# Squared-ReLU MLP of a hybrid trunk on one NeuronCore: its tile sums all on VectorE, adaLN dot products at other places

## The chip, the core and the metric

One core of a Trainium2 chip runs the whole kernel as one program. The engines are named as in the profile: PE (matrix), DVE (vector), ACT (scalar), POOL (GpSimd) and SP (its queue issues nearly all DMAs). The metric is the device time of one execution in microseconds (us); lower is better.

## The reference, cut to what matters

Two layers work on 1024 latent and 256 context tokens of width 1024. Layer 0 mixes tokens with latent attention, layer 1 with gated linear attention; each layer ends with the MLP. The second layer computes latent tokens alone behind its mixer.

```python
def sqrelu_mlp(h, w1, w2):                    # w1 1024 x 4096, w2 4096 x 1024
    return jnp.square(jax.nn.relu(h @ w1)) @ w2
m_lat = silu_c @ ada_w[i] + ada_b[i]          # 6 vectors of 1024 per layer: shift, scale, gate, twice
h = modulate(rms_norm(x_lat, norm_g[i, 2]), m_lat[:, 3], m_lat[:, 4])
x_lat = x_lat + m_lat[:, 5] * rms_norm(sqrelu_mlp(h, mlp_w1[i], mlp_w2[i]), norm_g[i, 3])
```

Everything is float32. The kernel writes each operand as a high part (a cast, fp32r) and a low part (operand minus high part), and multiplies with three matmuls: high by high, high by low, low by high (`mm3`, L232).

## The kernel before, in words

Activations lie transposed: 128 channels on the partitions, 512 tokens on the free side for each of the two latent blocks, 256 for the context. A tile of 128x512 floats has 256 KB. Weights, hidden tiles and the tiles of `ada_w` come by SP's DMA queue into 12 slots named `stg` (`load`, L212); ACT casts a high part (L204) and DVE or POOL subtracts it from the operand to get the low part (`sub`, L201). `tt` (L888) is the sum or difference of two tiles on the engine that it is given.

The MLP multiplies 2x2 blocks (two halves of the channels by two token blocks) with seven products instead of eight (Strassen's scheme in Winograd's form), so it needs sums of operands, of weights and of results.

`mlp` (L891) runs for each layer:

- `strassen_y` (L949) makes the sums T1 to T4 of the two latent blocks and splits them, in four steps.
- `up_first` (L978) computes the first two products of a pair of hidden tiles ahead, for the first 8 pairs of layer 0 and 11 of layer 1 (`early`), while the second block is still being made ready; the result waits in device memory.
- `up_pair` (L993) runs for each of 16 pairs. An early pair has five products of 12 matmuls (512 columns each), so 60 matmuls; the others have seven, and in layer 0 also the context's products. It makes the sums of weights s1, s2, a21, s2 again, splits five weight tiles (seven or eight in a pair that is not early), adds the products up out of PSUM (always on DVE), squares on ACT, and forms the low operands of the second matrix, t1, t2, c12 and t4, which go to device memory with the hidden tiles. `PLAN['up']` says for each of 16 such operations whether it runs on DVE (V) or POOL (P).
- After pair p, `ada_halves(PLAN['adah'][l][p])` (L257) does so many adaLN coefficients: two loads of 256 KB into `stg` slots, two products with a sum on DVE (L268), the sum of the two (L270), and bias and gain (L273). Its list holds 56 coefficients.
- `down` (L1068) multiplies with the second matrix in five products of 16 steps. In the first two (`w_first`, `w_s3`) a step also multiplies the context in layer 0 (`hc`): 12 matmuls of 512 and 12 of 256 columns. In the other three a step has 12 of 512. Loads and splits run two steps ahead. `ada_halves(1)` follows each step with `p % 3 == 0`.

As written, layer 0 takes 28 coefficients behind its pairs and the other 28 in the five products, so the list is empty before layer 1's MLP.

The order on every engine and on SP's queue is chosen by a list scheduler that simulates the engines' times when the kernel is built, in place of the order of the code; a changed engine or place may so shift the order of the work behind it.

Of the kernel before, what the change touches and what calls it, by code (L numbers as in the profile page):

```python
# [14 lines left out]
ALU = mybir.AluOpType  # L15
# [4 lines left out]
P = 128  # L20
# [70 lines left out]
 'pre': [1, 1, 0],  # L91
 'tk': [0.005, 0.64, 0.0064, 2.5, 1.024, 2.5],
 'gla': 'v2 s2 h2 h0 g0 v0 g2',
 'adah': [[0, 2, 3, 3, 2, 2, 2, 3, 2, 2, 2, 0, 0, 2, 2, 1], [0, 2, 2, 2, 2, 2, 2, 2, 2, 2, 2, 2, 2, 2, 2, 0]],
 'yield': [[[3.0, 6.0, 1.3, 8.0, 8.4, 1.3], [3.0, 8.4, 1.3, 8.0, 6.0, 1.3], [3.0, 6.0, 1.3, 8.0, 6.0, 1.3],
# [7 lines left out]
 'last': [3.0, 4.0, 1.3],  # L103
 'ladd': [3, 5, 6, 7],
 'up': [['VVPPVVVVVPPVVPPP', 'VVPPVVVPVVPVPPPP'], ['VVPVVVVPVVPPPPPP', 'PPPPVPPVVPVPPPPP']]}


def bits(ap):
# [3 lines left out]
class Trunk:  # L112
# [834 lines left out]
        self.nc.sync.dma_start(self.hidc_scr[f], self.sq_relu(ps, CTX))  # L947

    def strassen_y(self, ops, x, y):  # L949
        V, Pl, S = self.nc.vector, self.nc.gpsimd, ALU.subtract  # L950
        for k in range(4):
            t1, t2, t3, t4 = (self.t() for _ in range(4))
            self.tt(Pl, t1, y[k], x[k], S)
            self.tt(V, t2, y[k + 4], t1, S)
            self.tt(Pl, t3, y[k + 4], y[k], S)
            self.tt(Pl, t4, x[k + 4], t2, S)
            for n, t in (("22", y[k + 4]), ("T2", t2), ("T1", t1), ("T3", t3), ("T4", t4)):
                ops[n].append(self.msplit(t, 512, V))
            yield
# [32 lines left out]

    def up_pair(self, l, p, B, hc, early):  # L993
        nc, I = self.nc, self.I
        V, Pl = nc.vector, nc.gpsimd
        U = [Pl if x == 'P' else V for x in PLAN['up'][l][early]]
        if early:
            hc = None
        a11, a12 = (self.load(I["w1"][l, 2 * p, i]) for i in range(2))
        a21, a22 = (self.load(I["w1"][l, 2 * p + 1, i]) for i in range(2))  # L1000
        s1, s2 = self.slot("s", 512), self.slot("s", 512)
        w = {} if early else {"11": self.wsplit(a11, U[0]), "12": self.wsplit(a12, U[1])}
        self.tt(U[2], s1, a21, a22, ALU.add)
        self.tt(U[3], s2, s1, a11, ALU.subtract)
        w["S2"] = self.wsplit(s2, U[4])
        w["S1"] = self.wsplit(s1, U[5])
        if hc:
            w["21"] = self.wsplit(a21, U[6])
        self.tt(U[7], a21, a11, a21, ALU.subtract)
        w["S3"] = self.wsplit(a21, U[8])  # L1010
        w["22"] = self.wsplit(a22, U[9])
        self.tt(U[10], s2, a12, s2, ALU.subtract)
        w["S4"] = self.wsplit(s2, U[11])

        if early:
            c12, c11 = self.load(self.a_scr[l, p]), self.load(self.hid_scr[l][p, 0])
        else:
            c12, c11 = self.top_left(w, B)
        c22, c21 = self.t(), self.t()
        ps = self.product(w["S2"], B["T2"])  # L1020
        self.tt(V, c12, ps, c12, ALU.add)
        if hc:
            self.up_ctx_part(2 * p, (w["11"], w["12"]), hc)
        ps = self.product(w["S3"], B["T3"])
        self.tt(V, c21, ps, c12, ALU.add)
        ps = self.product(w["S1"], B["T1"])
        self.tt(V, c22, ps, c21, ALU.add)
        self.tt(V, c12, ps, c12, ALU.add)
        ps = self.product(w["S4"], B["22"])
        self.tt(V, c12, ps, c12, ALU.add)  # L1030
        if hc:
            self.up_ctx_part(2 * p + 1, (w["21"], w["22"]), hc)
        ps = self.product(w["22"], B["T4"])
        self.tt(V, c21, ps, c21, ALU.add)
        for c in (c22, c21, c12) if early else (c11, c22, c21, c12):
            self.square_relu(c)
        out = self.hid_scr[l][p]

        def put(i, x):
            nc.sync.dma_start(out[i], x)  # L1040

        t1, t2, t4 = self.t(), self.t(), self.t()
        if not early:
            put(0, c11)
        put(4, c22)
        put(5, c21)
        self.tt(U[12], t1, c12, c11, ALU.subtract)
        put(3, t1)
        self.tt(U[13], t2, c22, t1, ALU.subtract)
        put(1, t2)  # L1050
        self.tt(U[14], c12, c22, c12, ALU.subtract)
        put(2, c12)
        self.tt(U[15], t4, c21, t2, ALU.subtract)
        put(6, t4)

    def w2(self, l, f, i, tag="stg"):
# [11 lines left out]
    def down(self, l, C, yc):  # L1068


        nc = self.nc
        V = nc.vector
        keep, later = {}, []

        def part(p, r, i):
            return self.w2(l, 2 * p + r, i)

        def s3(p, a11):
            keep[p] = self.m()
            self.tt(V, keep[p], a11, part(p, 0, 1), ALU.subtract)  # L1080

        def s1(p, a21):
            self.tt(V, keep[p], a21, part(p, 1, 1), ALU.add)

        def w_first(p):
            a11 = part(p, 0, 0)
            w = self.wsplit(a11, V)
            s3(p, a11)
            return w, w

        def w_s3(p):
            w = self.wsplit(keep[p], V)
            a21 = part(p, 0, 1)
            s1(p, a21)
            return w, self.wsplit(a21, V) if yc is not None else None

        def w_s1(p):
            w = self.wsplit(keep[p], V)
            self.tt(V, keep[p], keep[p], part(p, 0, 0), ALU.subtract)
            return w, None  # L1100

        def w_s2(p):
            w = self.wsplit(keep[p], V)
            self.tt(V, keep[p], part(p, 1, 0), keep[p], ALU.subtract)
            return w, None

        def w_s4(p):
            return self.wsplit(keep.pop(p), V), None

        def copied(name):  # L1110
            def put(n, ps):
                C[name, n] = self.m()
                nc.scalar.copy(C[name, n], ps)
            return put

        def sums(n, ps):
            u = C["12", n] = self.m()
            self.tt(V, u, ps, C["11", n], ALU.add)
            later.extend(((C["u3", n], C["u3", n], u), (u, u, C["22", n]), (C["22", n], C["22", n], C["u3", n])))

        def last(n, ps):
            self.tt(V, C["12", n], ps, C["12", n], ALU.add)

        stages = ((w_first, 0, copied("11"), 0), (w_s3, 2, copied("u3"), 4), (w_s1, 3, copied("22"), None),
                  (w_s2, 1, sums, None), (w_s4, 4, last, None))
        steps = [(s, p) for s in stages for p in range(NP)]

        def prepare(s, p):
            (w, wc), hc = s[0](p), None
            b = self.msplit(self.load(self.hid_scr[l][p, s[1]]), 512, V)  # L1130
            if yc is not None and s[3] is not None:
                hc = self.msplit(self.load(self.hidc_scr[2 * p]), CTX, V)
            return w, b, wc, hc

        ready = [prepare(*x) for x in steps[:2]]
        for i, (s, p) in enumerate(steps):
            w, b, wc, hc = ready.pop(0)
            if i + 2 < len(steps):
                ready.append(prepare(*steps[i + 2]))
            if p == 0:  # L1140
                pss = [self.ps() for _ in range(4)]
                psc = [self.ps() for _ in range(2)] if hc else []
            for n in range(4):
                self.mm3(pss[n], self.cols(w, n * P), b, p == 0, p == NP - 1)
                if p == NP - 1:
                    s[2](n, pss[n])
            for n in range(4 if hc else 0):

                self.mm3(psc[n // 2][:, (n % 2) * CTX:(n % 2) * CTX + CTX], self.cols(wc, n * P), hc,
                         p == 0 and n % 2 == 0, p == NP - 1, True)  # L1150
                if p == NP - 1:
                    self.into_ctx(yc, s[3] + n, psc[n // 2][:, (n % 2) * CTX:(n % 2) * CTX + CTX])
            if p % 3 == 0:
                self.ada_halves(1)
            if later:
                self.tt(V, *later.pop(0), ALU.add)
# [508 lines left out]
```

## Time and profile before

| what | value |
|---|---|
| time, median of 3 runs | 2968.3 us (2967.92 to 2971.18) |
| profiled execution: time, span | 2972.39 us, 2970.6 us |
| mean granted clock of PE in it | 0.969 |
| busy share PE, DVE, ACT, POOL | 93%, 76%, 54%, 37% |
| DMA | 535.48 MB, mean 180 GB/s |

Busy time counts the union of an engine's instructions; neighbours on DVE overlap, so the pitch from start to start can be less than a duration. The granted clock is a share of full speed, 2.4 GHz; the lower level is 1.2 GHz. In time: layer 0's early pairs run from about 940 to 1100 us, its other pairs to 1290, the two products with the context to 1420, the other three to 1550; layer 1's early pairs from about 2390 to 2560, its other pairs to 2650, its five products to 2860.

### The profile page before, as it was taken

The page shows a single profiled execution, that of the slowest core. Times are in us where ns is not written, and L with a number is a line of the kernel's source. Part 1 is how long each engine was busy: PE and PEld are TensorE (multiplying, and loading weights), DVE is VectorE, ACT ScalarE, POOL GpSimd, SP SyncE. Part 2 cuts the span into 40 slices and gives each one's busy share as a digit, 9 for nine tenths or more (in the row PEclk, how much of TensorE's full clock was granted, in tenths as well). Part 3 has the DMA queues.
Part 4 walks back from the last instruction along what each step waited for, and adds up shares of the span by engine and source line. Part 5 has one row for each costly group of instructions (what it writes and reads, how often), then busy time and mean ns, then how long its engine had stood idle before and what let it go on. Part 6 is the DMA issues. An engine that isn't in the chain of part 4 may idle for free. (4 is left out here: it accounts for less than half of the span.)

```text
span 2970.6 us, 44564 instructions
## 1 busy us (share of the span) xinstructions
PE 2761.4 (93%) x14646; PEld 2358.3 (79%) x14646; DVE 2265.1 (76%) x4048; ACT 1603.6 (54%) x3360; POOL 1092.3 (37%) x757
## 2 busy tenths in 40 slices
PE   6799898999989889999999999799889999999997
PEld 4678887898778768888787888688887778788877
DVE  8898989887788985576878673466897876577666
ACT  4577665756555344444445464656655644555443
POOL 5554444522004763310002232356561289620012
PEclk8999999999999999999999999899999999999999
DMA  6221433324545774486765565667585647577454
GB/s 206 67 78 63 128 105 129 105 73 167 194 157 171 251 251 141 148 303 202 256 200 177 166 203 171 212 207 229 186 275 206 209 149 242 174 274 263 140 177 157
DMA packets 319384, 535.48 MB, mean 180 GB/s; under 512 B 33072, under 2 KB 96432, under 8 KB 319152
## 3 DMA queue, kind: packets, MB, share of 16 engines
q1 hardware_dynamic: 313328, 527.39, 54.0%
q10 hardware_dynamic: 5760, 5.25, 0.5%
q8 instruction: 115, 1.88, 0.3%
q14 instruction: 117, 0.96, 0.1%
q0 software_dynamic: 64, 0.00, 0.0%
HBM read 412.18 MB, written 120.32 MB: 179 GB/s over the span
## 5 line engine op out<-in xcount | busy, mean ns | idle before, releaser
L235 PE MATMUL ps<-m,w 128*128 128x512 f32 (+1 forms) x2320 | 906.7, 392 | 20.7 <-DVE m L201 20.2
L236 PE MATMUL ps<-m,w 128*128 128x512 f32 (+1 forms) x2320 | 899.2, 391 | 28.3 <-DVE w L201 22.5
L234 PE MATMUL ps<-m,w 128*128 128x512 f32 (+1 forms) x2320 | 891.4, 394 | 30.1 <-ACT m L204 13.2
L234 PEld LDWEIGHTS ps<-m,w 128*128 128x128 f32 x2320 | 445.1, 193 | 124.6 <-ACT m L204 18.9
L236 PEld LDWEIGHTS ps<-m,w 128*128 128x128 f32 x2320 | 445.5, 193 | 123.6 <-DVE w L201 28.3
L235 PEld LDWEIGHTS ps<-m,w 128*128 128x128 f32 x2320 | 447.1, 193 | 115.9 <-DVE m L201 28.1
L201 POOL TENSOR_TENSOR w<-stg,w 128x512 fp32r<-128x512 f32 (+2 forms) x157 | 220.4, 1406 | 818.5 <-ACT w L204 747.2
L204 ACT CAST w<-stg 128x512 fp32r<-128x512 f32 (+2 forms) x510 | 310.0, 615 | 310.0 <-PE ps L235 233.6
L201 DVE TENSOR_TENSOR w<-stg,w 128x512 fp32r<-128x512 f32 x353 | 280.5, 798 | 154.0 <-ACT w L204 136.5
L204 ACT CAST m<-stg 128x512 fp32r<-128x512 f32 x296 | 177.8, 625 | 153.6 <-DMA stg<-hid 139.7
L201 DVE TENSOR_TENSOR m<-stg,m 128x512 fp32r<-128x512 f32 x244 | 173.7, 724 | 55.1 <-ACT m L204 53.9
L234 PE MATMUL ps<-m,m 128*128 128x256 f32 (+1 forms) x632 | 187.3, 316 | 29.5 <-ACT m L204 18.6
L235 PE MATMUL ps<-m,m 128*128 128x256 f32 (+1 forms) x632 | 195.6, 311 | 10.4 <-POOL m L201 5.9
L234 PE MATMUL ps<-c,w 128*128 128x256 f32 (+1 forms) x664 | 186.4, 288 | 16.6 <-ACT c L436 7.1
L236 PE MATMUL ps<-m,m 128*128 128x256 f32 (+1 forms) x632 | 192.0, 305 | 1.8 <-DVE m L427 1.8
L235 PE MATMUL ps<-c,w 128*128 128x256 f32 (+1 forms) x664 | 185.4, 283 | 5.9 <-DVE c L437 3.5
L236 PE MATMUL ps<-c,w 128*128 128x256 f32 (+1 forms) x664 | 184.7, 283 | 0.0
L968 ACT ACTIVATE t<-t 128x512 f32<-128x512 f32 x109 | 68.8, 631 | 205.2 <-DVE t L889 197.6
L889 DVE TENSOR_TENSOR t<-ps,t 128x512 f32<-128x512 f32 x164 | 111.2, 684 | 86.2 <-PE ps L236 51.4
L234 PEld LDWEIGHTS ps<-m,m 128*128 128x128 f32 x632 | 123.7, 197 | 40.3 <-ACT m L204 20.2
L889 POOL TENSOR_TENSOR t<-t,t 128x512 f32<-128x512 f32 x82 | 124.3, 1525 | 73.0 <-DVE t L889 29.3
L234 PEld LDWEIGHTS ps<-c,w 128*128 128x128 f32 x664 | 125.4, 192 | 22.0 <-ACT c L436 7.5
(309 smaller groups left out, 6132.2 us busy)
## 6 DMA issues: line engine op xcount, KB each, us to landing
stg<-in_mlp_w SPq DMA_DIRECT2D x256, 256.0 KB, 4.0
stg<-hid SPq DMA_DIRECT2D x227, 256.0 KB, 3.7
hid<-t SPq DMA_DIRECT2D x205, 256.0 KB, 3.3
stg<-in_w SPq DMA_DIRECT2D x182, 256.0 KB, 3.2
ada<-in_adaT SPq DMA_DIRECT2D x88, 512.0 KB, 3.7
stg<-in_adaT SPq DMA_DIRECT2D x112, 256.0 KB, 3.7
stg<-in_gla_wv SPq DMA_DIRECT2D x64, 256.0 KB, 3.8
stg<-in_mla_wo SPq DMA_DIRECT2D x48, 256.0 KB, 4.4
```

Of the source, the lines that this page charges most:

```text
L201: eng.tensor_tensor(out=out, in0=a, in1=bits(hi), op=ALU.subtract)
L204: self.nc.scalar.copy(hi, src)
L234: mm(ps, lhs[0], rhs[0], start=first, stop=False, skip_group_check=shared)
L235: mm(ps, lhs[0], rhs[1], start=False, stop=False, skip_group_check=shared)
L236: mm(ps, lhs[1], rhs[0], start=False, stop=last, skip_group_check=shared)
L889: eng.tensor_tensor(out=out, in0=a, in1=b, op=op)
L968: self.nc.scalar.activation(c, c, AF.Relu)
```

## The change

Every sum of weights, every low half and every low operand of the first matrix runs on DVE, in `strassen_y` and in `up_pair` (the subtractions of L201 follow the engine given). `PLAN['up']` is gone. The dot products of layer 0's first eight pairs are gone, the last eight have two each, and in `down` one follows every step of a product with the context (32 in layer 0), none in the other three. Eight coefficients are left for layer 1, where pairs 1 to 4 take two each. In `down` of layer 1 the list is empty.

```diff
- 'adah': [[0, 2, 3, 3, 2, 2, 2, 3, 2, 2, 2, 0, 0, 2, 2, 1], [0, 2, 2, 2, 2, 2, 2, 2, 2, 2, 2, 2, 2, 2, 2, 0]],
+ 'adah': [[0, 0, 0, 0, 0, 0, 0, 0, 2, 2, 2, 2, 2, 2, 2, 2], [0, 2, 2, 2, 2, 2, 2, 2, 2, 2, 2, 2, 2, 2, 2, 0]],
- 'up': [['VVPPVVVVVPPVVPPP', 'VVPPVVVPVVPVPPPP'], ['VVPVVVVPVVPPPPPP', 'PPPPVPPVVPVPPPPP']]}
...
-            self.tt(Pl, t1, y[k], x[k], S)
+            self.tt(V, t1, y[k], x[k], S)
-            self.tt(Pl, t3, y[k + 4], y[k], S)
-            self.tt(Pl, t4, x[k + 4], t2, S)
+            self.tt(V, t3, y[k + 4], y[k], S)
+            self.tt(V, t4, x[k + 4], t2, S)
...
-        U = [Pl if x == 'P' else V for x in PLAN['up'][l][early]]
-        w = {} if early else {"11": self.wsplit(a11, U[0]), "12": self.wsplit(a12, U[1])}
-        self.tt(U[2], s1, a21, a22, ALU.add)
+        w = {} if early else {"11": self.wsplit(a11, V), "12": self.wsplit(a12, V)}
+        self.tt(V, s1, a21, a22, ALU.add)
... (U[3] to U[15] become V in the same way)
-            if p % 3 == 0:
+            if hc or yc is None and p % 3 == 0:
                 self.ada_halves(1)
```

## Rows read from the trace of the kernel before

**Rows 1.** The page, busy time and share of each engine, instructions.

```profile
PE 2761.4 (93%) x14646; PEld 2358.3 (79%) x14646; DVE 2265.1 (76%) x4048; ACT 1603.6 (54%) x3360; POOL 1092.3 (37%) x757
```

**Rows 2.** Stretches by stage; columns as in the first line.

```profile
core 0: us, PE busy (x) PEld busy (x) DVE busy (x) ACT busy (x) POOL busy (x), PEclk, DMA share, GB/s
940.00:1080.00 140.00, 121.39 (x492) 96.36 (x491) 126.57 (x211) 55.25 (x98) 96.73 (x61) 0.94 0.72 236
1100.00:1280.00 180.00, 179.65 (x950) 155.37 (x951) 107.67 (x182) 80.53 (x140) 64.12 (x46) 0.99 0.48 159
1290.00:1420.00 130.00, 126.90 (x720) 110.92 (x719) 88.47 (x191) 55.11 (x110) 3.37 (x1) 0.99 0.77 254
1420.00:1550.00 130.00, 127.18 (x559) 104.66 (x558) 111.07 (x237) 58.68 (x108) 1.28 (x1) 0.99 0.72 234
2380.00:2560.00 180.00, 170.80 (x723) 137.49 (x721) 120.36 (x140) 81.60 (x144) 156.07 (x108) 0.97 0.61 196
2660.00:2840.00 180.00, 180.00 (x796) 149.05 (x795) 126.68 (x198) 83.23 (x144) 0.00 (x0) 1.00 0.63 209
```

**Rows 3.** A stretch of 20 us in the first context product, same columns.

```profile
1340.00:1360.00 20.00, 20.00 (x118) 17.70 (x117) 10.12 (x21) 10.01 (x21) 0.00 (x0) 1.00 0.47 149
```

**Rows 4.** PE's waits, layer 0's early pairs (936 to 1100 us): total, times, longest.

```profile
PE ps L236 <- DVE w L201: 17.6, 8, 4.5
```

**Rows 5.** PE's waits in layer 1's early pairs, 2390 to 2560 us.

```profile
PE ps L236 <- POOL w L201: 5.8, 2, 4.4
```

**Rows 6.** Waits of SP's queue, 940 to 1100 us.

```profile
SPq L214 <- DVE y L268: 46.3, 32, 4.3
```

**Rows 7.** Waits of SP's queue, 1290 to 1420 us.

```profile
SPq L214 <- DVE y L268: 14.0, 15, 2.7
```

**Rows 8.** POOL in order of time: start, us, instruction.

```profile
1018.07 1.29 POOL L889 TENSOR_TENSOR stg<-stg,stg 128x512 f32<-128x512 f32 x1
```

**Rows 9.** DVE in order of time at the same place.

```profile
1018.10 1.81 DVE L268 CUSTOM_DVE_ANT_0 stg<-stg,cl 128x512 f32<-128x512 f32 x1 [2.49 <-DMA stg<-in_adaT]
```

**Rows 10.** DVE in order of time, POOL idle, third product of layer 0.

```profile
1494.69 0.69 DVE L201 TENSOR_TENSOR w<-m,w 128x512 fp32r<-128x512 f32 x1
1495.30 0.15 DVE L270 TENSOR_TENSOR m<-y 128x1 f32<-128x1 f32 x1
1495.37 0.69 DVE L201 TENSOR_TENSOR m<-stg,m 128x512 fp32r<-128x512 f32 x1
...
1497.78 0.69 DVE L268 CUSTOM_DVE_ANT_0 stg<-stg,cl 128x512 f32<-128x512 f32 x1
...
1498.39 0.69 DVE L201 TENSOR_TENSOR w<-m,w 128x512 fp32r<-128x512 f32 x1
...
1499.60 0.22 DVE L283 SCALAR_TENSOR_TENSOR m<-m,vec 128x1 f32<-128x1 f32 x1
1499.73 0.69 DVE L268 CUSTOM_DVE_ANT_0 stg<-stg,cl 128x512 f32<-128x512 f32 x1
```

**Rows 11.** DVE in order of time, first context product: a 256-column split.

```profile
1308.26 0.42 DVE L201 TENSOR_TENSOR c<-stg,c 128x256 fp32r<-128x256 f32 x1
1308.60 0.68 DVE L268 CUSTOM_DVE_ANT_0 stg<-stg,cl 128x512 f32<-128x512 f32 x1
```

**Rows 12.** Groups of DVE, 920 to 1100 us: busy, mean ns, idle before.

```profile
L268 DVE CUSTOM_DVE_ANT_0 stg<-stg,cl 128x512 f32<-128x512 f32 x46 | 47.5, 1042 | 16.7 <-DMA stg<-in_adaT 14.7 <-DMA hid<-t 1.8
L201 DVE TENSOR_TENSOR w<-s,w 128x512 fp32r<-128x512 f32 x27 | 26.3, 979 | 0.6 <-ACT w L204 0.4
```

**Rows 13.** DMA over 1290 to 1330 us.

```profile
DMA packets 8498, 13.90 MB, mean 348 GB/s; under 512 B 947, under 2 KB 2518, under 8 KB 8494
```

**Rows 14.** A group of POOL, 1100 to 1280 us (eight pairs of layer 0).

```profile
L889 POOL TENSOR_TENSOR t<-t,t 128x512 f32<-128x512 f32 x21 | 29.9, 1439 | 27.3 <-DVE t L889 14.0 <-issue 11.8 <-POOL t L889 1.5
```

More of the change, by code (lines that the diff above doesn't have):

```diff
@@ L103 @@
  'last': [3.0, 4.0, 1.3],
- 'ladd': [3, 5, 6, 7],
- 'up': [['VVPPVVVVVPPVVPPP', 'VVPPVVVPVVPVPPPP'], ['VVPVVVVPVVPPPPPP', 'PPPPVPPVVPVPPPPP']]}
+ 'ladd': [3, 5, 6, 7]}
 def bits(ap):
@@ L949, in strassen_y @@
     def strassen_y(self, ops, x, y):
-        V, Pl, S = self.nc.vector, self.nc.gpsimd, ALU.subtract
+        V, S = self.nc.vector, ALU.subtract
         for k in range(4):
             t1, t2, t3, t4 = (self.t() for _ in range(4))
-            self.tt(Pl, t1, y[k], x[k], S)
+            self.tt(V, t1, y[k], x[k], S)
             self.tt(V, t2, y[k + 4], t1, S)
-            self.tt(Pl, t3, y[k + 4], y[k], S)
-            self.tt(Pl, t4, x[k + 4], t2, S)
+            self.tt(V, t3, y[k + 4], y[k], S)
+            self.tt(V, t4, x[k + 4], t2, S)
             for n, t in (("22", y[k + 4]), ("T2", t2), ("T1", t1), ("T3", t3), ("T4", t4)):
@@ L994, in up_pair @@
         nc, I = self.nc, self.I
-        V, Pl = nc.vector, nc.gpsimd
-        U = [Pl if x == 'P' else V for x in PLAN['up'][l][early]]
+        V = nc.vector
         if early:
@@ L1001, in up_pair @@
         s1, s2 = self.slot("s", 512), self.slot("s", 512)
-        w = {} if early else {"11": self.wsplit(a11, U[0]), "12": self.wsplit(a12, U[1])}
-        self.tt(U[2], s1, a21, a22, ALU.add)
-        self.tt(U[3], s2, s1, a11, ALU.subtract)
-        w["S2"] = self.wsplit(s2, U[4])
-        w["S1"] = self.wsplit(s1, U[5])
-        if hc:
[L1008 to L1013, printed above, removed]
+        w = {} if early else {"11": self.wsplit(a11, V), "12": self.wsplit(a12, V)}
+        self.tt(V, s1, a21, a22, ALU.add)
+        self.tt(V, s2, s1, a11, ALU.subtract)
+        w["S2"] = self.wsplit(s2, V)
+        w["S1"] = self.wsplit(s1, V)
+        if hc:
+            w["21"] = self.wsplit(a21, V)
+        self.tt(V, a21, a11, a21, ALU.subtract)
+        w["S3"] = self.wsplit(a21, V)
+        w["22"] = self.wsplit(a22, V)
+        self.tt(V, s2, a12, s2, ALU.subtract)
+        w["S4"] = self.wsplit(s2, V)
         if early:
@@ L1046, in up_pair @@
         put(5, c21)
-        self.tt(U[12], t1, c12, c11, ALU.subtract)
+        self.tt(V, t1, c12, c11, ALU.subtract)
         put(3, t1)
-        self.tt(U[13], t2, c22, t1, ALU.subtract)
+        self.tt(V, t2, c22, t1, ALU.subtract)
         put(1, t2)
-        self.tt(U[14], c12, c22, c12, ALU.subtract)
+        self.tt(V, c12, c22, c12, ALU.subtract)
         put(2, c12)
-        self.tt(U[15], t4, c21, t2, ALU.subtract)
+        self.tt(V, t4, c21, t2, ALU.subtract)
         put(6, t4)
```

## The prediction

> **What bounds the kernel now.** The page first: PE is busy for 93% of the span, DVE for 76%, POOL for 37% [rows 1]. A change that takes no matmul away can move the time only where PE stands still or runs at the low clock. So the stretches by stage come next, and in them the count of matmuls, since PE's busy time is no rate. In layer 1's products, at full clock and with nothing idle, 796 matmuls of 512 columns take 180 us, 0.226 us each [rows 2]. By that pitch each stage has a loss, idle time and low clock together:
>
> - layer 0's early pairs, 940 to 1080 us: 140 - 492 x 0.226 = 28.8 us, clock 0.94 [rows 2];
> - layer 1's early pairs with their start, 2380 to 2560: 180 - 723 x 0.226 = 16.6 us [rows 2];
> - the products with the context, 1290 to 1420: 118 matmuls, half of each width, fill 20 us [rows 3], so a step of 24 takes 4.07 us; 720 are 30 steps, 122.1 us, and 7.9 us are lost [rows 2];
> - the other three products of layer 0: 130 - 559 x 0.226 = 3.7 us [rows 2] (the few narrower matmuls make it a little more);
> - the other pairs of layer 0, 1100 to 1280: PE busy for 179.65 of 180 us [rows 2], nothing to win.
>
> Then the waits: in layer 0's early pairs PE waited 17.6 us for low parts of weights from DVE [rows 4], in layer 1's 5.8 us for those of POOL [rows 5].
>
> **What a DVE operation costs.** With POOL idle a split is followed 0.61 us later by the next instruction, and 0.60 to 0.61 us separates neighbours although each lasts 0.69 [rows 10]: I count 0.605 us for a 128x512 operation, 0.34 for a 256-column one [rows 11], and for one adaLN coefficient two products of 0.61, a sum of 0.07 and a correction of 0.13 [rows 10], 1.42 us. Beside POOL it is otherwise: at 1018.07 POOL starts 1.29 us of work, DVE's product starts 0.03 us later and lasts 1.81 [rows 8, 9], that is until 0.55 us after POOL's end. In the early pairs the splits of sums average 0.979 us and the products 1.042 [rows 12]. POOL's work thus lengthens DVE's.
>
> **The change, part by part.**
>
> *Early pairs of layer 0.* An early pair has 5 splits, 4 sums of weights, 4 low operands and 6 sums out of PSUM on DVE: 19 x 0.605 = 11.5 us, against PE's 60 x 0.226 = 13.56. Now it holds 11 of these, stretched, and 17 coefficients over eight pairs; measured, 126.57 us for 492 matmuls are 15.4 us per pair [rows 2], more than PE's. The coefficients go from here, and with them 14.7 us in which DVE stood with a product at its head whose load was late [rows 12], and 46.3 us in which SP's queue waited for DVE to give back such a slot [rows 6], with the next weights behind it. What is late next is the chain sum, cast, split of a pair's first weights, and the start, where 12 operand sums (7.3 us) come to DVE. Bounds: the whole 28.8 us goes; or, if each pair gets the 3.4 us of waits on DVE that POOL had per pair in rows 14, DVE is at 14.9 instead of 15.4 us and 8 x 0.5 = 4 us go. I take 20, nearer the upper end, since the longest waits on DVE here were for the loads that go: -20 us.
>
> *Other pairs of layer 0.* 23 operations of 512 columns, two of 256 and two coefficients: 13.9 + 0.7 + 2.8 = 17.4 us of DVE per pair; eight pairs have 180 us of PE [rows 2], about 22.5 each. Hidden beside PE's matmuls: 0. Without that cover the seven operations from POOL would cost 4.2 us a pair.
>
> *Early pairs of layer 1.* POOL is at 156.07 of 180 us [rows 2] and PE's wait for it, 5.8 us [rows 5], goes. DVE has again 11.5 us per pair, 14.3 in the four pairs that get two coefficients: 0.8 us too much in each, and their loads take slots. Bounds: 16.6 us gained if all loss goes; or 4 us more lost than now (four pairs at 0.8, no gain). I take -2, near the second end, because the load on DVE there rises from 120.36/723 x 60 = 10.0 us per pair.
>
> *Products with the context.* 32 coefficients instead of 12. A step of the first product has three 512-wide operations and one narrow: 2.15 + 1.42 = 3.57 us of DVE against 4.07; of the second, four and one: 2.76 + 1.42 = 4.18, so 102%. A step loads 896 KB, and 512 KB with a coefficient: 1.44 MB, 46.1 MB in 32 steps; at 348 GB/s, reached over 40 us here [rows 13], 132.5 us, against PE's 130.2. But a step then takes six of twelve slots, and SP's queue already waits 14.0 us for products to return slots [rows 7]. Bounds: from below, all loss gone, -7.9; from above, the queue's mean rate of this stage, 254 GB/s [rows 2], 46.1 / 0.254 = 181.5 us, 51.3 over PE, +43 against now. I take 16 to 17 lost instead of 7.9, nearer the rate of rows 13, where the queue was kept full: +9 us.
>
> *Other three products of layer 0.* A step has three operations, 1.8 us, of PE's 2.7, with no coefficient left: 3.7 lost becomes about 1: -3 us.
>
> *Sum.* -20 - 2 + 9 - 3 = -16 us. The profiled execution took 2972.4 us (its span of 2970.6 and 1.8 around it), 4.1 over the median of the runs (2968.3); it becomes 2956.4, and a median about 2952.
>
> **A rule against it.** The Trainium skill (Perfetto Trace Analysis, Optimizing Scalar/DVE Operations) says that of a saturated DVE some work may well be given to another engine, even GPSIMD; this change does the reverse where DVE is busiest. The same place warns that the two share a read port, so that moving work between them may not help. This trace bears out the warning [rows 8, 9]; what the first half would make of the time is rival C.
>
> **The rivals.**
>
> *B, slower: the slots of the context products decide.* Queue and DVE wait on each other: a load needs a slot, a slot needs DVE's product, DVE waits in order for loads. If the queue gives no more than its present 254 GB/s [rows 2], the stage costs +43, and the sum is -25 + 43 = +18: 2986. It decides from where the stage loses 25 us more than now, a step of 5.1 us, 282 GB/s. For it: [rows 7]; against: [rows 13].
>
> *C, slower: DVE stays as slow per operation as now, and gets more.* Layer 0's early pairs: 15.4 + 8 x 0.605 - 2.1 x 1.42 = 17.3 us against 13.56, 30 us over eight pairs, nothing gained. Layer 1's: 10.0 + 9 x 0.605 + 1.0 = 16.4 us, 2.9 x 11 = 32 instead of 16.6 lost. +1 + 15 + 9 - 3 = +22: about 2990. Against it: durations fall to 0.69 as soon as POOL is idle [rows 10].
>
> *D, no change: waits move into DVE's line.* POOL's low operands waited 27.3 us in eight pairs [rows 14], 3.4 us a pair; there nobody stood behind them, on DVE the next pair's splits do. 11.5 us leave room for 2.1; at 2.7 us each of 19 early pairs loses 0.6, 12 us: 2964. For it: DVE runs in order; against: layer 0's early pairs lose such waits with their coefficients.
>
> *E, more:* all loss of rows 2's early pairs and three products goes, and the context stage stays as it is: -49, 2919.
>
> **How the numbers follow.** Chances: forecast 0.49 (own range 2938 to 2961), B 0.18, C 0.07, D 0.13, E 0.13. About 0.2%, 6 us, is what a measurement can tell from no change. Faster: forecast and E, 0.62 in all. Same: 0.13, most of D and the weak end of B. Slower: 0.25, the rest of B, C and D. The range 2925 to 2985 leaves out the far ends of E, B and C.
>
> **What would show it.** Right: POOL near 0 in the MLP's pairs; L201's w<-s near 0.69 us; over 85% as many matmuls per us in layer 0's early pairs as in rows 2's last stretch, now 79%; a context stage of 140 to 150 us with SP's waits for L268 doubled. Wrong: an early pair above 14.5 us (C or D), or a context step above 5.1 us (B).

## The result and the profile after

The changed kernel takes 2920.8 us (median of four runs, 2915.4 to 2923.2), the kernel before 2969.7 in the same series: a ratio of 0.983, 95% interval 0.981 to 0.985, and 0.983 again (0.982 to 0.985) in a second series of experiment 11. That is 49 us less where 16 were forecast, outside the range; it is the total that rival E priced at 2919. Medians are of fast runs; one execution of experiment 1, of 6949 us, is left out. The profiled executions are 57 us apart (2972.4 and 2915.4), since that of the changed kernel was the fastest of its runs; sums by stage go with these 57.

The busy time of the page, as in [rows 1]:

```profile
PE 2746.1 (94%) x14646; PEld 2354.7 (81%) x14646; DVE 2313.1 (79%) x4331; ACT 1603.9 (55%) x3360; POOL 664.0 (23%) x474
```

DVE has 283 instructions more and POOL 283 fewer, but DVE's busy time grew by only 48 us, 0.17 us for each.

The stretches that answer to [rows 2] (layer 0's early pairs; the products with the context, from the last hidden tile of the context to the last copy of the second product; the three others; layer 1's early pairs; behind the first, part of layer 0's other pairs):

```profile
core 0: us, PE busy (x) PEld busy (x) DVE busy (x) ACT busy (x) POOL busy (x), PEclk, DMA share, GB/s
940.00:1080.00 140.00, 140.00 (x653) 117.24 (x652) 123.77 (x228) 66.56 (x119) 0.00 (x0) 1.00 0.67 219
1100.00:1250.00 150.00, 150.00 (x799) 129.70 (x798) 112.18 (x221) 67.22 (x120) 0.00 (x0) 1.00 0.55 180
...
1253.00:1396.00 143.00, 140.94 (x794) 121.91 (x793) 125.51 (x322) 64.38 (x130) 0.00 (x0) 1.00 0.93 316
...
1386.00:1516.00 130.00, 129.76 (x574) 107.26 (x575) 91.73 (x151) 59.90 (x108) 3.20 (x3) 1.00 0.56 185
2340.00:2520.00 180.00, 178.68 (x777) 146.21 (x776) 164.64 (x293) 90.92 (x156) 0.00 (x0) 0.99 0.69 227
```

In layer 0's early pairs PE is never idle and at full clock; before it lost a fifth of the time. (The early pairs now end sooner, so the 653 matmuls hold narrower ones of the pairs behind them.) POOL is at 0. DVE's groups there, 940 to 1080 us, answer to [rows 12] (line numbers are one or two lower in the changed kernel):

```profile
L200 DVE TENSOR_TENSOR w<-s,w 128x512 fp32r<-128x512 f32 x27 | 18.3, 681 | 1.1 <-ACT w L203 1.1
...
L267 DVE CUSTOM_DVE_ANT_0 stg<-stg,cl 128x512 f32<-128x512 f32 x13 | 8.9, 689 | 3.6 <-DMA stg<-in_adaT 3.4
```

0.979 us has become 0.681 and 1.042 has become 0.689. (The 13 products belong to later pairs.) SP's waits for these products to return a slot, in 940 to 1080 us, are 13.0 us, where [rows 6] had 46.3 over a slightly longer stretch; in the products with the context they fell from the 14.0 of [rows 7] to 4.9, though there are more than twice as many of them. First the early pairs', then the context stage's:

```profile
SPq L213 <- DVE y L267: 13.0, 10, 2.8
```

```profile
SPq L213 <- DVE y L267: 4.9, 17, 0.9
```

To see where the 57 us are, some events of the program that both have serve as marks: the first and the last time that a tile is written or read. Each line has them behind its durations ("first to last start"). Kernel before:

```profile
L984 SPq DMA_DIRECT2D hid<-t x19: 319/327/433, 852.6 to 2384.7; - x19
L947 SPq DMA_DIRECT2D hidc<-t x32: 319/379/2222, 872.6 to 1289.3; - x32
L1246 ACT COPY m<-ps x8: 363/377/397, 1349.7 to 1431.3; 128x256 f32<-128x256 f32 x8
L214 SPq DMA_DIRECT2D s<-x_scr x48: 319/424/1112, 1530.7 to 2889.6; - x48
L982 SPq DMA_DIRECT2D a_scr<-t x19: 319/326/461, 847.7 to 2376.8; - x19
L1040 SPq DMA_DIRECT2D hid<-t x186: 319/370/1951, 966.0 to 2648.5; - x186
```

The changed kernel:

```profile
L983 SPq DMA_DIRECT2D hid<-t x19: 319/320/385, 854.5 to 2336.4; - x19
L946 SPq DMA_DIRECT2D hidc<-t x32: 319/382/848, 874.9 to 1253.5; - x32
L1244 ACT COPY m<-ps x8: 360/376/405, 1316.0 to 1395.7; 128x256 f32<-128x256 f32 x8
L213 SPq DMA_DIRECT2D s<-x_scr x48: 319/427/1667, 1489.1 to 2834.0; - x48
L981 SPq DMA_DIRECT2D a_scr<-t x19: 319/320/446, 849.6 to 2332.1; - x19
L1038 SPq DMA_DIRECT2D hid<-t x186: 319/327/2132, 963.9 to 2596.4; - x186
```

Between these marks:

| stretch | from, to | before | after | difference | forecast |
|---|---|---|---|---|---|
| layer 0's first matrix | first hid, last hidc | 436.7 | 399.0 | -37.7 | -20 |
| products with the context | last hidc, last copy L1246 | 142.0 | 142.2 | +0.2 | +9 |
| the other products, end of layer 0 | that, first read of x_scr | 99.4 | 93.4 | -6.0 | -3 |
| layer 1's mixer and start of its MLP | that, last a_scr | 846.1 | 843.0 | -3.1 | 0 |
| layer 1's pairs | that, last hid | 271.7 | 264.3 | -7.4 | -2 |

Up to the first mark the changed kernel is 1.9 us later. The 3.1 us of layer 1's mixer, where nothing was changed, stay open. Behind the last mark it is 4.9 us shorter, but those belong to layer 1's pairs: the mark is a store that comes from DVE's line, and that line now runs further behind PE. Counted by PE's own work, the same matmuls in the same mix of widths, the early pairs are these (columns as above): 750 matmuls of layer 0, before and after; 794 of layer 1, before, after, and in run 8 below, which leaves no coefficient to layer 1:

```profile
925.50:1118.50 193.00, 169.82 (x750) 137.42 (x749) 166.51 (x277) 78.41 (x141) 125.29 (x81) 0.94 0.69 225
```

```profile
928.20:1084.50 156.30, 156.30 (x750) 131.82 (x749) 140.05 (x257) 74.19 (x134) 0.00 (x0) 1.00 0.65 212
```

```profile
2368.50:2568.50 200.00, 187.75 (x794) 150.77 (x793) 136.48 (x154) 95.28 (x170) 174.75 (x120) 0.97 0.60 193
```

```profile
2323.90:2511.70 187.80, 184.14 (x794) 149.02 (x793) 173.75 (x314) 94.69 (x163) 0.00 (x0) 0.99 0.67 222
```

```profile
2324.10:2507.10 183.00, 181.44 (x794) 148.12 (x794) 165.22 (x271) 94.62 (x164) 0.00 (x0) 1.00 0.65 211
```

So layer 0's early pairs gained 36.7 us, nearly all of its stretch's 37.7, and layer 1's 12.2, not 7.4.

### The profile page after: what moved, and what is told of

It reads as the page before. It is cut to its first block, busy times and chain, and to the rows that moved or that the text cites. A ratio compares the mean times of both kernels' runs of the same rounds, so it can differ in the third digit from the quotient of the medians.

```text
span 2913.6 us, 44354 instructions
## 1 busy us (share of the span) xinstructions
PE 2746.1 (94%) x14646; PEld 2354.7 (81%) x14646; DVE 2313.1 (79%) x4331; ACT 1603.9 (55%) x3360; POOL 664.0 (23%) x474
## 5 line engine op out<-in xcount | busy, mean ns | idle before, releaser
L234 PE MATMUL ps<-m,w 128*128 128x512 f32 (+1 forms) x2320 | 897.5, 388 | 13.2 <-DVE m L200 13.2
L233 PE MATMUL ps<-m,w 128*128 128x512 f32 (+1 forms) x2320 | 882.2, 390 | 25.2 <-ACT m L203 14.5
L235 PE MATMUL ps<-m,w 128*128 128x512 f32 (+1 forms) x2320 | 889.7, 387 | 2.1 <-DVE w L200 2.0
L200 POOL TENSOR_TENSOR w<-stg,w 128x512 fp32r<-128x512 f32 (+2 forms) x138 | 194.1, 1409 | 1706.2 <-ACT w L203 1648.3
L233 PEld LDWEIGHTS ps<-m,w 128*128 128x128 f32 x2320 | 439.4, 190 | 118.8 <-ACT m L203 21.8
L234 PEld LDWEIGHTS ps<-m,w 128*128 128x128 f32 x2320 | 442.0, 191 | 103.8 <-DVE m L200 18.3
L235 PEld LDWEIGHTS ps<-m,w 128*128 128x128 f32 x2320 | 440.1, 190 | 91.6 <-DVE w L200 4.4
L200 DVE TENSOR_TENSOR w<-stg,w 128x512 fp32r<-128x512 f32 x372 | 273.1, 738 | 142.6 <-ACT w L203 127.8
L233 PE MATMUL ps<-m,m 128*128 128x256 f32 (+1 forms) x632 | 187.9, 316 | 28.7 <-ACT m L203 17.7
L234 PE MATMUL ps<-m,m 128*128 128x256 f32 (+1 forms) x632 | 198.0, 315 | 7.4 <-DVE m L200 4.1
L235 PE MATMUL ps<-m,m 128*128 128x256 f32 (+1 forms) x632 | 194.9, 310 | 2.4 <-DVE m L426 2.4
L233 PEld LDWEIGHTS ps<-m,m 128*128 128x128 f32 x632 | 124.0, 197 | 39.8 <-ACT m L203 19.7
L203 ACT CAST w<-m 128x512 fp32r<-128x512 f32 x128 | 79.2, 622 | 117.1 <-PE ps L234 116.9
L234 PEld LDWEIGHTS ps<-m,m 128*128 128x128 f32 x632 | 125.2, 198 | 17.6 <-POOL m L200 5.5
```

The source lines that it names most:

```text
L200: eng.tensor_tensor(out=out, in0=a, in1=bits(hi), op=ALU.subtract)
L203: self.nc.scalar.copy(hi, src)
L233: mm(ps, lhs[0], rhs[0], start=first, stop=False, skip_group_check=shared)
L234: mm(ps, lhs[0], rhs[1], start=False, stop=False, skip_group_check=shared)
L235: mm(ps, lhs[1], rhs[0], start=False, stop=last, skip_group_check=shared)
```

## The experiments

Two theories stood against each other. P: POOL's work lengthened DVE's. S: the dot products' late loads and the slots that they held were the loss. Below, "layer 0's stretch" and "layer 1's stretch" are the first and last row of the table, read in each trace from the same marks; for layer 1 the text gives the count by matmuls beside it.

| run | median us | ratio to before, 95% | layer 0's stretch | context products | layer 1's stretch |
|---|---|---|---|---|---|
| 1, sums on DVE alone | 2927.6 | 0.987 (0.985 to 0.990) | 415.9 | 140.9 | 262.6 |
| 2, dot products moved alone | 2947.8 | 0.994 (0.991 to 0.996) | 406.6 | 141.0 | 281.0 |
| 3, POOL reads 512 columns | 2995.7 | 1.009 (1.007 to 1.012) | 446.1 | 142.2 | 299.4 |
| 4, POOL reads 16 columns | 2913.0 | 0.982 (0.979 to 0.984) | 398.8 | 144.0 | 262.8 |
| 5, early loads | 2923.7 | 0.984 (0.982 to 0.986) | 404.2 | 141.6 | 264.0 |
| 6, early DVE work | 2930.2 | 0.987 (0.984 to 0.989) | 412.3 | 141.5 | 263.9 |
| 7, POOL writes only | 2919.3 | 0.983 (0.981 to 0.985) | 398.6 | 137.8 | 263.4 |
| 8, none in layer 1 | 2909.4 | 0.980 (0.977 to 0.982) | 401.0 | 139.5 | 261.8 |
| 9, context: more DVE work | 2939.7 | 0.990 (0.988 to 0.993) | 397.6 | 155.9 | 263.8 |
| 10, context: more loads | 2938.4 | 0.989 (0.985 to 0.993) | 401.0 | 154.8 | 263.9 |

**1 and 2: each half alone.** The first is the changed kernel with the list and the condition of before:

```diff
- 'adah': [[0, 0, 0, 0, 0, 0, 0, 0, 2, 2, 2, 2, 2, 2, 2, 2], ...
+ 'adah': [[0, 2, 3, 3, 2, 2, 2, 3, 2, 2, 2, 0, 0, 2, 2, 1], ...
-            if hc or yc is None and p % 3 == 0:
+            if p % 3 == 0:
```

> All sums and low halves on DVE as in the changed kernel; the adaLN dot products at their old places (17 behind layer 0's early pairs, one behind every third step of the five products). Theory P (POOL's work lengthened DVE's operations in the early pairs, and that was the loss): most of the 49 us between the two kernels is here, 2920 to 2932 us. DVE then has 11.5 us plus 2.1 x 1.42 = 14.5 us per early pair of layer 0 against PE's 13.56, some 8 us lost there, nothing else. Theory S (the dot products' late loads and their slots were the loss): at most the 6 us of PE's waits for POOL in layer 1 come back, 2955 to 2968 us, and SP's queue still waits some 46 us for L268 between 940 and 1100 us.

The second is the kernel before with the opposite two lines.

> The other half alone: dot products moved as in the changed kernel, the sums divided between DVE and POOL as before. Theory P: an early pair of layer 0 still has DVE operations of about 1 us beside POOL, 11 of them against 13.56 us of PE, so it falls under PE's time and part of the loss goes, 2945 to 2962 us; layer 1's pairs with coefficients get slower. Theory S: the early pairs of layer 0 run at PE's rate, 38 us earlier at their end as in the changed kernel, 2925 to 2938 us.

Their stretches of 940 to 1080 us, columns as above, first the one with all sums on DVE, then the one with the dot products moved:

```profile
940.00:1080.00 140.00, 128.58 (x562) 104.35 (x561) 131.98 (x295) 57.90 (x101) 0.00 (x0) 0.98 0.76 251
```

```profile
940.00:1080.00 140.00, 135.17 (x615) 111.88 (x615) 107.98 (x155) 68.99 (x119) 106.32 (x71) 0.99 0.65 216
```

In the same order, PE's wait for DVE in 940 to 1100 us, and for the second run its splits of sums in 940 to 1080:

```profile
PE ps L233 <- DVE t L888: 8.6, 4, 3.9
```

```profile
PE ps L236 <- DVE w L201: 2.4, 1, 2.4
L201 DVE TENSOR_TENSOR w<-s,w 128x512 fp32r<-128x512 f32 x27 | 26.7, 993 | 5.0 <-ACT w L204 5.0
```

By the total time both fall where P had them. By stage neither theory is whole. In layer 0's stretch sums on DVE alone bring 20.8 us and moved dot products alone 30.1, together 37.7: the halves overlap. Run 1 takes away most of DVE's excess but not all of it: 131.98 us for 562 matmuls are 14.1 for the 60 of a pair, against PE's 13.56. In the second run DVE's splits are still lengthened (w<-s at 0.993 us), yet DVE, at 108 of 140 us, has room, and PE waited for DVE's low parts for 2.4 us in one place, against [rows 4]'s 17.6. Some 7 us of loss stay, though (163.5 us for the 750 matmuls counted above, against 156.3). In layer 1 only P's half gains, 9.1 us by the marks and 17.0 by matmuls (183.0 us, as run 8), and coefficients beside divided sums cost 9.3 by the marks, 12.5 by matmuls.

**3, 4 and 7: what of POOL's work holds DVE up.** In every pair POOL does extra work whose results nobody reads, in three forms:

```diff
+        for hi, lo in w.values():      # run 3; run 4 has 16 in place of 512
+            self.tt(nc.gpsimd, s1[:, :512], bits(hi)[:, :512], bits(lo)[:, :512], ALU.add)
+        for _ in w:                    # run 7
+            nc.gpsimd.memset(s1, 0.0)
```

> The changed kernel, and in every pair of the first matrix POOL adds the high and low part of each split weight tile (512 columns, five per early pair), into the tile of s1, which nobody reads any more: extra work, its results unused. Theory P: DVE's operations with two operands in SBUF are stretched again beside these, by about 0.5 us for each of POOL's, 2.5 us on 11.5 per early pair; with the waits the early pairs lose 5 to 25 us: 2926 to 2946 us, and w<-s averages over 0.85 us. If the port does nothing: 2921 us, w<-s at 0.69.

> The control for it: the same additions on POOL with the same waits, but on 16 columns of 512, so that POOL holds nothing for long. Theory P: 2918 to 2925 us, as the changed kernel. If it was the waits and longer-held weight and s tiles that cost time beside wide POOL work, and not the port, this one is as slow as with 512 columns.

> The changed kernel, and POOL sets the tile of s1 to zero once for every split weight tile (five times per early pair, 512 columns), when nobody reads it any more: POOL writes SBUF and reads nothing; extra work, unused. If only POOL's reads hold up DVE's operations with two operands in SBUF: 2913 to 2924 us, w<-s at 0.68 us as in the changed kernel. If any POOL work on SBUF does, as the wide additions did: 2930 us or more, w<-s over 0.75.

DVE in 940 to 1080 us beside wide reads:

```profile
L200 DVE TENSOR_TENSOR w<-s,w 128x512 fp32r<-128x512 f32 x24 | 20.1, 843 | 0.0
L200 DVE TENSOR_TENSOR w<-stg,w 128x512 fp32r<-128x512 f32 x18 | 18.6, 1043 | 0.0
L888 DVE TENSOR_TENSOR stg<-ps,stg 128x512 f32<-128x512 f32 x24 | 16.2, 678 | 0.0
```

POOL there, and then POOL in the run that only writes, with DVE's splits beside it:

```profile
L888 POOL TENSOR_TENSOR s<-w,w 128x512 f32<-128x512 f32 x42 | 66.3, 1579 | 72.6 <-DVE w L200 69.4 <-DVE m L282 2.0
```

```profile
L1014 POOL MEMSET s<- 128x512 f32 x48 | 25.3, 527 | 115.5 <-DVE w L200 113.2
```

```profile
L200 DVE TENSOR_TENSOR w<-s,w 128x512 fp32r<-128x512 f32 x27 | 18.3, 683 | 1.2 <-ACT w L203 1.2
```

Reads of 512 columns lengthen DVE's splits, which have two SBUF operands, to 0.84 and 1.04 us on average, leave its additions with a PSUM operand at 0.678, and cost 75 us, far more than the 5 to 25 expected for the early pairs: my sum had 0.5 us for each of five, but DVE's room beside PE in an early pair is only 2 us (13.56 less 11.5), and both layers lost, 47 us in layer 0's stretch and 35 in layer 1's. The same waits with 16 columns cost nothing, nor does POOL when it writes without reading. So it is the reading, and not POOL's being late with tiles. Write-only work was shorter (0.53 against 1.58 us an instruction), but that is not why: in run 7's trace, from 930 to 2650 us, 31 splits of weights overlap one of the writes in time, and they take 0.685 us on average and 0.693 at most. In run 3 the 82 that overlap an addition take 1.27 us, and in run 4 the 43 that do 0.76.

**5 and 6: what of a dot product costs in an early pair.** Extra, unused work behind (5) and in (6) layer 0's early pairs:

```diff
+            if ctx and p < early:      # run 5
+                for i in range(4):
+                    w = self.load(self.I["adaT"][0, 40 + p][:, (i % 2) * 512:(i % 2) * 512 + 512])
+                    self.nc.vector.tensor_copy(self.tiny(1), w[:, 0:1])
+        if early and l == 0:           # run 6
+            for _ in range(5):
+                self.tt(V, s1, s1, s1, ALU.add)
```

> The changed kernel with, behind each of layer 0's eight early pairs, the four loads of two adaLN coefficients and on DVE only a copy of one column of each: the loads and slots of the old place without its arithmetic; extra work, unused. In the changed kernel the stretch from the first hidden tile written to the last context hidden tile of layer 0 takes 399 us, in the kernel with everything on DVE and the dot products at their old places 416, before 437. Theory S (loads and slots cost): 407 to 416 us here. Theory D (DVE's time costs): 399 to 402.

> The changed kernel with five more additions on DVE in each early pair of layer 0 (3.0 us, as much as two coefficients), no loads; results unused. DVE has then 14.5 us per pair against PE's 13.56, 0.97 us too much. Theory D: that stretch takes 407 us or more (8 x 0.97 = 8 over 399). Theory S: under 404, since DVE's lead from the start covers part of it.

Loads, with their copies of one column, cost 5.2 us, between what S (loads and slots) and D (DVE's time; not rival D) said; DVE's time alone 13.3, as D said, and more than its sum of 8. Together 18.5, near the 16.9 of run 1. The stretch of 940 to 1080 us with more DVE work shows DVE at 133 of 140 us and PE at 593 matmuls, not 653:

```profile
940.00:1080.00 140.00, 130.24 (x593) 106.02 (x593) 133.37 (x237) 60.18 (x105) 0.00 (x0) 1.00 0.57 190
```

So of a dot product's cost in this stretch DVE's time is the larger part and its loads are the smaller, and both S and D hold in part.

**9 and 10: how near the context stage was to its bounds.** With each coefficient of these steps, more of one kind of work:

```diff
+                if more:               # run 9, for each half of a coefficient
+                    self.tt(nc.vector, self.t(), w, self.cl[:, h], ALU.add)
+                if more:               # run 10
+                    w2 = self.load(self.I["adaT"][l, m * KT + k][:, h])
+                    nc.vector.tensor_copy(self.tiny(1), w2[:, 0:1])
```

> The changed kernel with two more additions on DVE for every coefficient in the products with the context of layer 0 (1.21 us per step, no load; results unused). From the last context hidden tile written to the last copy of the context's second product the changed kernel takes 142 us. DVE has then 4.8 us per step of the first product and 5.4 of the second, 163 us in 32 steps against PE's 130. If DVE's time bounds the stage as soon as its sum exceeds PE's: 165 to 178 us there. If the slots and the queue were the near bound, as the prediction had it: the same or more, with SP waiting for DVE most.

> The changed kernel with two more loads of 256 KB for every coefficient in the products with the context of layer 0, of which DVE copies one column each: eight of twelve slots and 1.97 MB per step, 62.9 MB in all; results unused. If the queue can give only the 322 GB/s of this stage in the changed kernel: 195 us for the stage, against 142. If it gives the 371 GB/s of that kernel's first 40 us there: 170 us. If slots bound it (8 of 12 per step, no two steps ahead): over 200 us and a rate under 300 GB/s.

The stage in either, first with DVE's work, then with the loads:

```profile
1254.00:1410.00 156.00, 143.46 (x786) 122.01 (x785) 153.65 (x374) 62.60 (x124) 0.00 (x0) 0.99 0.86 280
```

```profile
1250.00:1405.00 155.00, 142.30 (x772) 120.70 (x772) 130.46 (x376) 62.72 (x124) 0.00 (x0) 0.99 1.04 379
```

Both cost 13 to 14 us in the stage, under what was expected. With more work DVE is busy for 153.65 of 156 us, so there DVE bounds it; my 163 us of work did not all fall between the two marks, for the stretch up to the first read of x_scr grew by another 6 us. With more loads the queue moved 379 GB/s for 155 us, and no single wait of SP's was over 1.4 us. The slots, which the prediction feared, are not the near bound: the queue keeps full with eight of twelve taken in a step.

**8, 11 and 12: a version faster than both.** Three coefficients behind each of layer 0's last eight pairs, none in layer 1:

```diff
- 'adah': [[0, 0, 0, 0, 0, 0, 0, 0, 2, 2, 2, 2, 2, 2, 2, 2], [0, 2, 2, 2, ...
+ 'adah': [[0, 0, 0, 0, 0, 0, 0, 0, 3, 3, 3, 3, 3, 3, 3, 3], [0] * 16],
```

> The changed kernel with three coefficients behind each of layer 0's last eight pairs, so that none is left for layer 1. Layer 0's pairs have DVE work of 18.8 us against some 22.5 of PE and stay hidden; layer 1's early pairs lose the 2 us that the two versions with all sums on DVE differ by there (264.3 and 262.6 us from the last tile of the first products to the last hidden tile). Theory that this is DVE's and the slots' cost: 2915 to 2920 us against 2921, at the edge of what can be told. If the products' order alone: 2921.

> The changed kernel once more, timed beside the version without coefficients in layer 1 on one chip: 2915 to 2922 us if the first measurement holds.

> The version with three coefficients behind each of layer 0's last eight pairs and none in layer 1, timed again beside the changed kernel. If its 2909 us was that placement (layer 1's pairs 2.5 us shorter in its profile, and layer 0's 2 us longer): 0 to 3 us below the changed kernel here. If it was the spread between runs: within 3 us on either side.

Timed again beside each other, the changed kernel has 2919.7 us, ratio 0.983 (0.982 to 0.985), and this version 2910.8, ratio 0.980 (0.978 to 0.981): the intervals don't touch, so it is faster, by about 9 us. That is more than the expected 0 to 3. Its profile shows layer 1's early pairs 4.8 us shorter by matmuls (183.0 against 187.8; 2.5 by the marks) and layer 0's stretch 2.0 longer. The two profiled executions are only 4.4 us apart, 1.7 in the second series, so where the rest of the 9 us lies is open.

## Why the prediction was wrong

- **What bounds the kernel: right.** PE's idle time in the early pairs, from DVE being over PE's time, was the place; the sign and the mechanism hold. The stretch from [rows 8, 9], that a DVE operation with two SBUF operands ends after POOL's, is shown by runs 3, 4 and 7.
- **Early pairs of layer 0: the step that failed most.** "I take 20", of a loss of 28.8 us. 36.7 us went: the whole loss, and the bound itself was too small, since it was read off 940 to 1080 us and the early pairs lost time up to about 1105. The price per operation was right (splits at 0.68 in place of 0.98), DVE came out under PE's time, and then nothing of the loss stays: the prediction gave no reason to keep a third of it. Half measures (runs 1 and 2) each give more than half of it.
- **Products with the context: the second step that failed.** +9 forecast, +0.2 measured. The upper bound took 254 GB/s for what the queue can give; it was only what was asked of it. It gave 316 here and 379 in run 10. And 102% of DVE in a step of the second product was judged by itself, though DVE has 88% in the first and two steps of lead; over both it is 3.57 and 4.18 against twice 4.07, 95%.
- **Early pairs of layer 1: the third step that failed.** -2 forecast, -12.2 measured by matmuls. "Near the second end, because the load on DVE there rises": but it rises to 11.5 us a pair, still under PE's 13.56, and then the loss goes as in layer 0. Without coefficients there (runs 1 and 8) 17.0 of 20.6 us went (200.0 less 794 x 0.226). The four pairs with coefficients cost 4.8 us of that; priced at 3.2, they were not what was wrong.
- **The other three products:** -6.0 in a stretch that also holds the end of layer 0, where -3 was forecast, nearly the whole loss of [rows 2].
- **Other pairs of layer 0:** right, PE is busy for 150.00 of 150 us beside DVE's added work, from 1100 to 1250 us (run 8 adds still more; its layer 0 stretch is 2.0 us longer).
- **The rivals.** B is refuted by the stage's 142.2 us and by run 10, C by the durations of 0.68. D's waits do show in run 1 (PE waited 8.6 us for sums that DVE had not got to), where DVE has 14.5 us a pair, and not in the changed kernel. E met the total and had 0.13, but partly by luck: it had 28.8 us for layer 0's early pairs, where 36.7 went, and 16.6 for layer 1's, where 12.2 did, and the two misses offset each other. All terms were set too near their bad ends at once; those of the pairs hung on one thing, whether DVE falls below PE's time, and so were not apart from each other. The signs of being right nearly all came (only SP's waits fell where they were to double) and none of being wrong: they told the forecast from B, C and D, but not from E.

## What to carry to other kernels

Here a stage that lost time because one engine was a little over the bounding engine's need lost little or nothing once that engine was under it (0 in layer 0's early pairs, 3.6 of 20.6 us in layer 1's without coefficients; 7 stayed in run 2, where POOL still had its half). So ask pair by pair whether the engine falls under, and forecast most of the loss or none. Count it between two events of the program, not between round times, and by the bounding engine's own work: a mark on another engine's line hid 5 us here. Work on POOL that reads SBUF isn't free for DVE: 283 operations more on DVE, taken from POOL, cost it 48 us of busy time where their pitch alone makes 171. A rate seen in a stage is what was asked for, until something else is seen to wait for it.

## What the runs showed of the hardware

- Beside POOL's reads DVE's splits, with two SBUF operands, take 0.84 to 1.04 us instead of 0.68, and POOL's work is longer too (1.58 us on average in run 3; 1.29 for the one in [rows 8]). Beside POOL's writes they do not (0.683 us, run 7; 0.693 at most for the 31 that overlap one). The Trainium skill (SBUF — State Buffer, Who interferes with whom) says the same: two SBUF inputs on DVE contend with a GpSimd instruction that reads SBUF, not with one that only writes; these traces agree.
- The DMA queues moved 379 GB/s over 155 us (run 10), and 371 over the first 40 us of the context products after the change:

```profile
DMA packets 8851, 14.84 MB, mean 371 GB/s; under 512 B 981, under 2 KB 2269, under 8 KB 8847
```

  The Trainium skill (SBUF — State Buffer, Summary: rules for kernel authors) counts with about 358 GB/s between device memory and SBUF; here more was measured, and the measurement decides.
